# Three more weight remainders taken from PSUM, one weight copy moved ahead of the first convolution tap, a Silu moved behind a bank copy, loads issued ahead of stores, and one matrix's operand parts prepared a pair earlier

## The chip, the cores and the metric

The kernel runs on one core of a Trainium2 chip. The metric is device time in microseconds for one execution. A core has five instruction queues that run beside each other and wait for each other through semaphores: PE (TensorE, matrix products), DVE (VectorE), ACT (ScalarE), POOL (GpSimd) and SP (SyncE, which here issues all transfers of the steady part). Each queue runs its instructions in the order in which they were issued. Matrix products go into PSUM, which has eight banks of 128 x 512 float32 values; everything else lives in SBUF or in device memory.

## The reference

The input x has 1024 rows of 1024 float32 values. With one layer only the gated short convolution runs:

```python
def short_conv_mixer(u, w_in, conv_w, w_out):
    z, bg, cg, v = jnp.split(u @ w_in.astype(u.dtype), 4, axis=-1)
    y = bg * causal_dwconv(cg * v, conv_w) * jax.nn.silu(z)
    return y @ w_out.astype(u.dtype)

u = rms_norm(h, pre_norm[i])
h = h + rms_norm(m, post_norm[i])
```

w_in is 1024 x 8192 (four parts of 2048 columns), the causal convolution has three taps and works on each of the 2048 columns by itself, and w_out is 2048 x 1024. All of it is float32.

## The kernel before, in words

The kernel works transposed: columns of the projection lie on the 128 partitions and the 1024 positions lie along the free dimension. It has a start (normalisation, transposes, the operands made from u), a long first phase (the input projection, the gates and the convolution) and a second phase (the output projection and the last norm). The change touches the first phase.

**Channels and pairs.** The 2048 branch columns are sixteen channels c = 0 to 15 of 128 columns. A channel is two pairs: the even pair p = 2c is (CG, V), the odd pair p = 2c + 1 is (Z, BG). A pair is a 2 x 2 block product over halves of the contraction and halves of the positions, done by a seven-product scheme, products a to g. A product is four contraction tiles times three matmuls (low part of the weight by high part of the operand, high by low, high by high), so twelve matmuls of 128 x 512, in `product` (L221 to L223).

**Seven products inside.** From channel 3 on, product b, and for channels 4 to 14 product f too, is itself replaced by seven half-size products a' to g' (`deep_product`, L780 to L782, six matmuls of 128 x 256 each). `by_seven` says where: "f" from DEEP_F = 4 to channel 14. The half-size operands of f, c', e', d' and g', are made once from the operand of f, in three steps: `deep_parts` (L701, POOL adds the high and low part), `deep_subs` (L707 to L710, POOL subtractions) and `deep_split` (a copy to the high part on ACT, a subtraction to the low part on DVE, L160 and L161). The table UNDER says behind which product of which pair each step is issued.

**Splitting weights.** Each weight is split into a high part and a remainder. `split` copies on ACT (L160, L168) and subtracts on DVE with both inputs in SBUF (L161, L187). `split_by_bank` (L181 to L183) does one more ACT copy, of the source into one fixed PSUM bank named `beside`, and DVE subtracts with that bank as its first input. There is only one such bank, so the next ACT copy into it waits until DVE has read the last one. `split_w` and BY_BANK_DEEP choose between the two; names are wa to wg for the weights of a pair (dwb0 to dwb2, dwf0 to dwf2 for the half-size ones), with h or l behind for the two parts.

**What sets the order.** The list `slots` is the order of products on PE. Behind each product the loop issues, by hand, the splits of the weights that are due within LEAD = 7.0 us of planned time (`prepare`), then the reading of the bank (`after`, `deep_after`, `deep_after_f`), then loads, sums on POOL and the table UNDER. Every engine's order follows from this one program order. In an odd pair of channels 4 to 14 PE's order is c; c' and e' of f; e; f' of b and of f; d' of b and of f; d; g' of b and of f; then product a of the next pair; then g.

**What reads a bank.** Products a, c, d and g of a pair share one bank (px). Behind a and c, ACT copies the bank to SBUF (`snap`, L229), and PE may go on with the bank only then. Behind d, DVE adds the bank to a copy (L248), and g waits for that. In the half-size products DVE reads the banks at L787, L802, L812 and L816.

**Around the first tap.** Behind d' of b in an odd pair, `deep_after` adds the bank (L787), `gate` writes the gated input (L271, DVE), and `first_tap` scales it on ACT (L657). The two other taps are `conv_tap` (L666, DVE). Behind g' of f, `deep_after_f` adds the bank (L802, DVE), applies Silu (L806, ACT) and multiplies (L807, POOL). Behind a of the following even pair, ACT copies the bank (L229) and applies Silu to the other half (L1061).

**Stores and loads on SP.** `add_t` prepares the output projection's weights: DVE subtractions (L345, L332 to L340), each followed by a store that waits for it. `fetch_t` loads them, and `fetch_s` loads an earlier channel's result y for `add_y` (L302 to L304, from channel 9 on). TODO says at which pair which of these is done; before, it covers pairs 8 to 23, that is channels 4 to 11.

Of the kernel before, what the change touches and what calls it, by code (L numbers as in the profile page):

```python
# [17 lines left out]
DEEP_F = 4  # L18
LEAD = 7.0
BY_BANK_DEEP = (("b", 0), ("b", 1), ("f", 0))  # L20
# [3 lines left out]
def kernel(  # L24
# [16 lines left out]
    nc = tc.nc  # L41
# [147 lines left out]
    def split_w(p, kinds):  # L189
        for i in kinds if p < len(PAIRS) else "":  # L190
            if i in ("ag" if p % 2 else "adg") and by_seven("f", p // 2):
                wt[p, i] = [page(f"w{i}{h}_{p}", F32R) for h in "hl"]
                split_by_bank(source(p, i), *wt[p, i])
                continue
            split_high(p, i)
            split_low(p, i)
# [587 lines left out]
    def deep_after(c, i):  # L784
# [3 lines left out]
        if i == "d'":  # L788
            if by_seven("f", c):
                gate(c)  # L790
                first_tap(c)
            else:
                start_conv(c, lambda: third_unit(1) if c == NC - 1 else None)

    def deep_after_f(c, i):
# [4 lines left out]
        if i in ("b'", "g'"):  # L800
            t, v_ = (t0, banks[p, "v"]) if i == "b'" else (t1, banks[p + 1, "v"])
            nc.vector.tensor_add(t, v_, t)  # L802
            if i == "b'":
                nc.gpsimd.tensor_mul(g[:, :HH], t[:, :HH], sn[p, "e"][:, :HH])
            else:
                nc.scalar.activation(t, t, AF.Silu)  # L806
                nc.gpsimd.tensor_mul(cvs[c][:, HB:], t, sn[p + 1, "e"])  # L807
# [126 lines left out]
    TODO = {2 * DEEP_F + 2 * j + n: j + n * CH for j in range(CH) for n in (0, 1)}  # L934
# [3 lines left out]
    for p in range(2, len(PAIRS)):  # L938
# [32 lines left out]
        ("d", 2 * DEEP_F - 2): lambda: deep_parts("f", [0]),  # L971
        ("f", 2 * DEEP_F - 2): lambda: deep_parts("f", [2]),
        ("g", 2 * DEEP_F - 2): lambda: deep_parts("f", [1]),
        ("c", 2 * DEEP_F - 1): lambda: deep_parts("f", [3]),
        ("e", 2 * DEEP_F - 1): lambda: deep_subs("f", [0]),
        ("f", 2 * DEEP_F - 1): lambda: deep_subs("f", [1]),
        ("c", 2 * DEEP_F): lambda: deep_split("f", "c'"),
        ("d", 2 * DEEP_F): lambda: deep_split("f", "e'"),
        ("a", 2 * DEEP_F + 1): lambda: deep_split("f", "d'"),
        ("g", 2 * DEEP_F): lambda: deep_split("f", "g'"),  # L980
# [21 lines left out]
    for n, slot in enumerate(slots):  # L1002
# [21 lines left out]
        if i == "c":  # L1024
            if p % 2 and p // 2 < DEEP:
                nc.scalar.activation(sn[p, "a"], sn[p, "a"], AF.Silu)
            if p % 2 == 0 and p in TODO:
                add_t(TODO[p], [0, 1])
                fetch_t(TODO[q])
            if p % 2 == 0 and p > 2:  # L1030
                fetch_s(prev)
            if p % 2 == 0 and p // 2 >= DEEP:
# [26 lines left out]
        elif i == "a":  # L1059
            if prev >= 0 and p % 2 == 0 and by_seven("f", prev):  # L1060
                nc.scalar.activation(sn[p - 1, "a"], sn[p - 1, "a"], AF.Silu)  # L1061
# [264 lines left out]
```

## Time and profile before

| | us |
|---|---|
| median of three runs | 819.88 (818.24 to 820.08) |
| profiled execution | 818.51 |
| its span on the core | 816.7 |
| PE busy in the span | 780.3 (96%) |
| DVE busy | 675.2 (83%) |
| ACT busy | 399.6 (49%) |
| POOL busy | 401.9 (49%) |

The profile lists every instruction with its start and duration in microseconds from the start of the span. A bracket at the end of a row says how long the engine had been idle before it and what ended that. Matmuls overlap each other, so a matmul's own duration is longer than the distance to the next one; the pace of PE is read from the starts. "PEclk" is the share of full clock that TensorE was granted.

### The profile page before, as it was taken

The page shows a single profiled execution, that of the slowest core. Times are in us where ns is not written, and L with a number is a line of the kernel's source. Part 1 is how long each engine was busy: PE and PEld are TensorE (multiplying, and loading weights), DVE is VectorE, ACT ScalarE, POOL GpSimd, SP SyncE. Part 2 cuts the span into 40 slices and gives each one's busy share as a digit, 9 for nine tenths or more (in the row PEclk, how much of TensorE's full clock was granted, in tenths as well). Part 3 has the DMA queues.
Part 4 walks back from the last instruction along what each step waited for, and adds up shares of the span by engine and source line. Part 5 has one row for each costly group of instructions (what it writes and reads, how often), then busy time and mean ns, then how long its engine had stood idle before and what let it go on. Part 6 is the DMA issues. An engine that isn't in the chain of part 4 may idle for free.

```text
span 816.7 us, 11954 instructions
## 1 busy us (share of the span) xinstructions
PE 780.3 (96%) x4050; PEld 663.9 (81%) x4050; DVE 675.2 (83%) x964; ACT 399.6 (49%) x742; POOL 401.9 (49%) x337
## 2 busy tenths in 40 slices
PE   8999999998899999999898899999999999999997
PEld 6888888887787878787787777878787889989985
DVE  6899658979797979797978797768687899996885
ACT  7655425254445454445343443544544555855831
POOL 2516679678374747474645463838374210530031
PEclk9999999999999999999999999999999999999999
DMA  9212240515272717272828271415150989786445
GB/s 312 51 52 60 83 141 1 181 61 179 76 230 74 251 53 251 63 240 79 276 60 265 83 251 53 143 52 157 37 180 32 307 289 369 280 262 204 153 154 182
DMA packets 115822, 127.18 MB, mean 156 GB/s; under 512 B 7416, under 2 KB 74032, under 8 KB 115760
## 3 DMA queue, kind: packets, MB, share of 16 engines
q1 hardware_dynamic: 115744, 126.41, 47.9%
q8 instruction: 32, 0.52, 0.3%
q14 instruction: 30, 0.25, 0.1%
q10 hardware_dynamic: 16, 0.00, 0.0%
HBM read 91.78 MB, written 34.60 MB: 155 GB/s over the span
## 4 chain that ended last, share of the span: by engine, by line
PE 62%; DVE 19%; issue 9%; POOL 4%; ACT 4%; DMA 3%; DVEq 0%; POOLq 0%; SPq 0%; ACTq 0%
PE px L221 8%; PE px L222 7%; PE px L223 7%; PE po_x L1115 4%; PE po_x L1116 4%; PE po_x L1117 4%; PE pv L221 3%; PE pv L223 3%; PE pv L222 3%; DVE cv L666 3%; DMA s<-y_d 2%; DVE t L345 1%; ACT beside L182 1%; DVE sna L787 1%; DVE wel L187 1%
## 5 line engine op out<-in xcount | busy, mean ns | idle before, releaser
L252 POOL TENSOR_TENSOR sne<-sne,cv 128x512 f32<-128x512 f32 x15 | 20.9, 1393 | 156.8 <-DVE cv L666 147.6
L221 PE MATMUL px<-u_c,wcl 128*128 128x512 f32 x124 | 49.7, 401 | 12.8 <-DVE wcl L187 6.7
L182 ACT COPY beside<-raw 128x512 f32<-128x512 f32 x66 | 38.9, 589 | 28.4 <-DVE dwb1l L183 16.6
L187 DVE TENSOR_TENSOR wel<-se,weh 128x512 fp32r<-128x512 f32 x31 | 37.0, 1193 | 19.1 <-ACT weh L168 19.1
L229 ACT COPY snc<-px 128x512 f32<-128x512 f32 x31 | 18.2, 586 | 69.7 <-PE px L223 69.7
L221 PE MATMUL px<-u_g,wgl 128*128 128x512 f32 x124 | 49.4, 398 | 2.7 <-DVE sne L248 2.7
L154 POOL TENSOR_TENSOR sc<-se,raw 128x512 f32<-128x512 f32 x31 | 49.5, 1596 | 2.6 <-POOL se L152 0.2
L152 POOL TENSOR_TENSOR se<-raw,raw 128x512 f32<-128x512 f32 x31 | 45.4, 1463 | 10.6 <-DMA raw<-in_sc_w_in 6.3
L221 PE MATMUL px<-u_d,wdl 128*128 128x512 f32 x124 | 49.3, 398 | 0.0
L148 POOL TENSOR_TENSOR raw<-raw,raw 128x512 f32<-128x512 f32 x31 | 49.3, 1590 | 0.0
L221 PE MATMUL pv<-u_e,wel 128*128 128x512 f32 x124 | 48.6, 392 | 0.7 <-DVE wel L187 0.7
L156 POOL TENSOR_TENSOR sf<-raw,sc 128x512 f32<-128x512 f32 x31 | 49.1, 1583 | 0.0
L222 PE MATMUL px<-u_d,wdh 128*128 128x512 f32 x124 | 48.9, 395 | 0.0
L223 PE MATMUL px<-u_d,wdh 128*128 128x512 f32 x124 | 48.8, 393 | 0.0
L221 PE MATMUL px<-u_a,wal 128*128 128x512 f32 x124 | 48.6, 392 | 0.0
L222 PE MATMUL px<-u_a,wah 128*128 128x512 f32 x124 | 48.5, 391 | 0.0
L222 PE MATMUL px<-u_g,wgh 128*128 128x512 f32 x124 | 48.5, 391 | 0.0
L223 PE MATMUL px<-u_c,wch 128*128 128x512 f32 x124 | 48.4, 390 | 0.0
L222 PE MATMUL pv<-u_e,weh 128*128 128x512 f32 x124 | 48.4, 390 | 0.0
L223 PE MATMUL px<-u_g,wgh 128*128 128x512 f32 x124 | 48.3, 390 | 0.0
L222 PE MATMUL px<-u_c,wch 128*128 128x512 f32 x124 | 48.3, 389 | 0.0
L223 PE MATMUL pv<-u_e,weh 128*128 128x512 f32 x124 | 48.3, 389 | 0.0
(535 smaller groups left out, 2766.1 us busy)
## 6 DMA issues: line engine op xcount, KB each, us to landing
raw<-in_sc_w_in SPq DMA_DIRECT2D x128, 256.0 KB, 4.2
y_d<-cv SPq DMA_DIRECT2D x16, 512.0 KB, 3.0
s_d<-s SPq DMA_DIRECT2D x32, 256.0 KB, 4.4
t<-in_sc_w_out SPq DMA_DIRECT2D x32, 256.0 KB, 3.3
t_d<-t SPq DMA_DIRECT2D x32, 256.0 KB, 2.4
tb<-in_sc_w_out SPq DMA_DIRECT2D x16, 256.0 KB, 3.9
s<-y_d SPq DMA_DIRECT2D x16, 256.0 KB, 4.7
xr<-in_x SPq DMA_DIRECT2D x16, 256.0 KB, 4.0
```

The source lines that it names most:

```text
L148: nc.gpsimd.tensor_sub(t, block(p, 0, 0), t)
L152: nc.gpsimd.tensor_add(t, block(p, 1, 0), block(p, 1, 1))
L154: nc.gpsimd.tensor_sub(t, sums[p, "e"], block(p, 0, 0))
L156: nc.gpsimd.tensor_sub(t, block(p, 0, 1), sums[p, "c"])
L182: nc.scalar.copy(b, src)
L187: nc.vector.tensor_sub(lo, source(p, i), hi.bitcast(F32))
L221: nc.tensor.matmul(ps, lo, UH[i][:, k], start=first and k == 0, stop=False, skip_group_check=True)
L222: nc.tensor.matmul(ps, hi, UL[i][:, k], start=False, stop=False, skip_group_check=True)
L223: nc.tensor.matmul(ps, hi, UH[i][:, k], start=False, stop=last, skip_group_check=True)
L1115: nc.tensor.matmul(ps, lo, u[:, 0, k], start=first, stop=False, skip_group_check=True)
L1116: nc.tensor.matmul(ps, hi, u[:, 1, k], start=False, stop=False, skip_group_check=True)
L1117: nc.tensor.matmul(ps, hi, u[:, 0, k], start=False, stop=last, skip_group_check=True)
```

## The change

Five edits, all in the order or the kind of the small work around the matmuls; PE's own order of products stays the same.

1. The remainders of dwb2, dwf2 and of wd in odd pairs, in channels 4 to 14, are made by `split_by_bank` in place of `split`. Each has one more ACT copy, and DVE reads PSUM.
2. The weight wg of an odd pair in channels 4 to 14 is split ahead of `gate` and `first_tap`; before, it came behind `first_tap`.
3. The Silu behind g' of f and the POOL product behind it are issued behind the copy of the bank of the next pair's product a.
4. In even pairs from `TODO`, `fetch_t` and `fetch_s` are issued ahead of `add_t`, and TODO begins two pairs (one channel) later: pairs 10 to 25.
5. The steps that make f's half-size operands are issued earlier: the sums on POOL in pairs 5 to 7, the splits behind products e, d, f and g of pair 7, in channel 3 (before, the sums in pairs 6 and 7, the splits in pairs 8 and 9, in channel 4).

```diff
-BY_BANK_DEEP = (("b", 0), ("b", 1), ("f", 0))
+BY_BANK_DEEP = (("b", 0), ("b", 1), ("b", 2), ("f", 0), ("f", 2))
...
-            if i in ("ag" if p % 2 else "adg") and by_seven("f", p // 2):
+            if i in "adg" and by_seven("f", p // 2):
...
             if by_seven("f", c):
+                split_w(2 * c + 1, "g")
                 gate(c)
                 first_tap(c)
...
-            else:
-                nc.scalar.activation(t, t, AF.Silu)
-                nc.gpsimd.tensor_mul(cvs[c][:, HB:], t, sn[p + 1, "e"])
             return
...
-    TODO = {2 * DEEP_F + 2 * j + n: j + n * CH for j in range(CH) for n in (0, 1)}
+    TODO = {2 * DEEP_F + 2 + 2 * j + n: j + n * CH for j in range(CH) for n in (0, 1)}
...
-        ("d", 2 * DEEP_F - 2): lambda: deep_parts("f", [0]),
-        ("f", 2 * DEEP_F - 2): lambda: deep_parts("f", [2]),
-        ("g", 2 * DEEP_F - 2): lambda: deep_parts("f", [1]),
-        ("c", 2 * DEEP_F - 1): lambda: deep_parts("f", [3]),
-        ("e", 2 * DEEP_F - 1): lambda: deep_subs("f", [0]),
-        ("f", 2 * DEEP_F - 1): lambda: deep_subs("f", [1]),
-        ("c", 2 * DEEP_F): lambda: deep_split("f", "c'"),
-        ("d", 2 * DEEP_F): lambda: deep_split("f", "e'"),
-        ("a", 2 * DEEP_F + 1): lambda: deep_split("f", "d'"),
-        ("g", 2 * DEEP_F): lambda: deep_split("f", "g'"),
+        ("d", 2 * DEEP_F - 3): lambda: deep_parts("f", [0]),
+        ("f", 2 * DEEP_F - 3): lambda: deep_parts("f", [2]),
+        ("d", 2 * DEEP_F - 2): lambda: deep_parts("f", [1]),
+        ("f", 2 * DEEP_F - 2): lambda: deep_parts("f", [3]),
+        ("g", 2 * DEEP_F - 2): lambda: deep_subs("f", [0]),
+        ("c", 2 * DEEP_F - 1): lambda: deep_subs("f", [1]),
+        ("e", 2 * DEEP_F - 1): lambda: deep_split("f", "c'"),
+        ("d", 2 * DEEP_F - 1): lambda: deep_split("f", "e'"),
+        ("f", 2 * DEEP_F - 1): lambda: deep_split("f", "d'"),
+        ("g", 2 * DEEP_F - 1): lambda: deep_split("f", "g'"),
...
             if p % 2 == 0 and p in TODO:
-                add_t(TODO[p], [0, 1])
                 fetch_t(TODO[q])
             if p % 2 == 0 and p > 2:
                 fetch_s(prev)
+            if p % 2 == 0 and p in TODO:
+                add_t(TODO[p], [0, 1])
...
             if prev >= 0 and p % 2 == 0 and by_seven("f", prev):
-                nc.scalar.activation(sn[p - 1, "a"], sn[p - 1, "a"], AF.Silu)
+                for t in (sn[p - 1, "c"], sn[p - 1, "a"]):
+                    nc.scalar.activation(t, t, AF.Silu)
+                nc.gpsimd.tensor_mul(cvs[prev][:, HB:], sn[p - 1, "c"], sn[p - 1, "e"])
```

## The prediction

> **What bounds the kernel now.** First PE's own list of waits, for a queue that is busy nearly throughout (us in total, times, longest).
>
> ```profile
> PE pv2f L780 <- DVE snc L816: 10.3, 7, 2.6
> PE px L221 <- DVE wcl L187: 6.7, 4, 2.3
> PE px L221 <- ACT sna L229: 6.0, 8, 0.8
> PE px L221 <- DVE sne L248: 2.7, 6, 0.7
> ```
>
> PE waits for late readers of a bank and for late remainders on DVE and ACT, and for little else. Then the stretches of channel 4, of 5 to 8, 9 to 11, 12, and 13 with 14, cut where product c of an even pair starts (length; PE, PEld, DVE, ACT, POOL busy; granted clock, DMA share, GB/s), and from the timeline the pace of matmuls that wait for nothing.
>
> ```profile
> 176.03:221.15 45.12, 39.60 (x205) 33.90 (x204) 39.77 (x57) 20.91 (x42) 28.75 (x26) 0.96 0.42 137
> 221.15:379.79 158.64, 152.52 (x817) 129.40 (x815) 137.70 (x197) 75.54 (x141) 93.07 (x77) 1.00 0.49 156
> 379.79:508.63 128.84, 117.68 (x613) 100.15 (x613) 109.16 (x154) 56.99 (x106) 69.14 (x58) 0.97 0.50 161
> 508.63:547.96 39.33, 37.92 (x206) 32.32 (x205) 29.52 (x44) 19.06 (x36) 21.53 (x20) 1.00 0.33 101
> 547.96:626.17 78.21, 75.86 (x408) 64.64 (x408) 58.69 (x87) 37.63 (x70) 43.91 (x39) 1.00 0.33 101
> sum 450.14, PE 423.58 PEld 360.40 DVE 374.85 ACT 210.14 POOL 256.38; mean PE 84.72 PEld 72.08 DVE 74.97 ACT 42.03 POOL 51.28
> ```
>
> ```profile
> 173.31 0.39 PE L221 MATMUL px<-u_g,wgl 128*128 128x512 f32 x1
> 176.03 0.39 PE L221 MATMUL px<-u_c,wcl 128*128 128x512 f32 x1
> ...
> 252.00 0.28 PE L780 MATMUL px2b<-ubgh_deep,dwb 128*128 128x256 f32 x1
> 252.35 0.28 PE L780 MATMUL px2b<-ubgh_deep,dwb 128*128 128x256 f32 x1
> ```
>
> A whole product, twelve matmuls, takes 176.03 - 173.31 = 2.72 us, and three half-width matmuls 0.35. A channel is ten products and 84 half-width matmuls: 27.2 + 9.9 = 37.1 us if PE waits for nothing. Eleven channels need 408.1 and take 450.1: 42.0 us are loss, 8.0 of it in channel 4, 10.2 in 5 to 8, 17.5 in 9 to 11, 2.2 in 12, 4.0 in 13 and 14. That is all that this change can win; PE's order stays, and so does the work of the start and of the second phase.
>
> **Silu and the tap (edits 2 and 3).** The turn from channel 5 to 6, in the timeline (start, us, engine, line; idle before and its end in brackets):
>
> ```profile
> 250.79 1.15 ACT L657 ACTIVATE cv<-gpad,cw 128x1024 f32<-128x1024 f32 x1 [3.01 <-issue]
> 252.97 0.69 DVE L183 TENSOR_TENSOR wgl<-beside,wgh 128x512 fp32r<-128x512 f32 x1 [2.26 <-ACT beside L182]
> 255.97 0.69 DVE L248 TENSOR_TENSOR sne<-px,sne 128x512 f32<-128x512 f32 x1
> 256.71 0.50 PE L221 MATMUL px<-u_g,wgl 128*128 128x512 f32 x1 [0.40 <-DVE sne L248]
> 258.81 0.63 ACT L806 ACTIVATE snc<-snc 128x512 f32<-128x512 f32 x1 [5.32 <-DVE snc L802]
> 259.86 0.58 ACT L229 COPY sna<-px 128x512 f32<-128x512 f32 x1
> 260.49 0.50 PE L221 MATMUL px<-u_c,wcl 128*128 128x512 f32 x1 [0.75 <-ACT sna L229]
> ```
>
> ACT stands 5.32 us at the Silu, and the bank copy that PE needs stands behind it. Product a ended before g began, over 3 us earlier; with the Silu behind the copy, PE doesn't wait. By the list that is 6.0 us in eight waits, and each costs PE some 0.16 more between starts: 7.3 us. Silu and the POOL product land 1 to 2 us later than the copy, and only the store of y waits for them; DVE's half of y is later still.
>
> ACT also idles 3.01 us ahead of the tap, so the two copies of wg (0.6 each) fit in there. DVE's gate comes 0.69 us later, the tap with it, but the 2.26 us of waiting for `beside` go: L248 at 255.97 would come some 1.6 us sooner, more than PE's wait of 0.40. Six such waits, 2.7 us in the list, 3.7 with the restarts, go. If the tap came later by more than that, they would stay.
>
> **Three more through PSUM (edit 1).** The groups of instructions by form (count, busy, mean ns):
>
> ```profile
> L161 DVE TENSOR_TENSOR dwf2l<-dsf,dwf2h 128x512 fp32r<-128x512 f32 x11 | 18.5, 1678 | 0.0
> L161 DVE TENSOR_TENSOR dwb2l<-dsb,dwb2h 128x512 fp32r<-128x512 f32 x13 | 17.7, 1358 | 0.0
> L187 DVE TENSOR_TENSOR wdl<-raw,wdh 128x512 fp32r<-128x512 f32 x20 | 25.7, 1287 | 4.5 <-ACT wdh L168 4.5
> L183 DVE TENSOR_TENSOR wdl<-beside,wdh 128x512 fp32r<-128x512 f32 x11 | 7.6, 691 | 7.4 <-ACT beside L182 7.4
> ```
>
> DVE saves 1.68 + 1.36 + 1.29 - 3 x 0.69 = 2.3 us a channel; ACT does three copies more, about 0.58 each as the bank copy at 259.86, 1.7 us, at half load. But the three follow each other, and one bank serves them: behind the first subtraction ACT makes the next copy, the snap of c, wdh and the third copy, each about 0.6, with the second subtraction beside them, so the third ends about 0.69 + 4 x 0.6 + 0.69 = 3.8 us after the first starts. Now channel 10:
>
> ```profile
> 432.33 0.86 SPq L289 DMA_DIRECT2D s<-y_d  x2
> 439.31 0.69 DVE L302 TENSOR_TENSOR s<-s,cv 128x512 f32<-128x512 f32 x1 [1.83 <-DMA s<-y_d]
> 442.61 0.47 PE L221 MATMUL px<-u_c,wcl 128*128 128x512 f32 x1 [2.17 <-DVE wcl L187]
> 446.92 1.44 DVE L161 TENSOR_TENSOR dwb2l<-dsb,dwb2h 128x512 fp32r<-128x512 f32 x1
> 452.01 0.41 DVE L816 TENSOR_TENSOR snc<-pv2f,snc 128x256 f32<-128x256 f32 x1
> 452.47 0.39 PE L780 MATMUL pv2f<-u_f,dwf2l 128*128 128x256 f32 x1 [1.97 <-DVE snc L816]
> ```
>
> The bank reader that PE waits for comes 452.01 - 446.92 = 5.1 us behind the first of the three; with 3.8 for them and 0.34 for the reader in between, 4.1. So each pv2f wait shrinks by 0.95. The longest of the seven, 2.6, is channel 4's and goes with the work that leaves it; of the three near 1.97 in channels 9 to 11 about 1.0 is left, 1.15 with the restart; the rest, 10.3 - 2.6 - 5.9 = 1.8 in channels 6 to 8, all but goes. Bounds: by busy time alone 2.3 a channel is won and these waits end; with the copies standing behind DVE's backlog nothing is won. I take the row of channel 10.
>
> **Loads ahead of stores (edit 4).** s<-y_d was issued at 432.33 behind two stores that waited for L345; it can go some 4 us earlier, and the 1.83 us wait at L302 ends. DVE then makes wcl 1.83 sooner, and 0.34 of PE's 2.17 is left. Of the 6.7 us of wcl waits 2.3 are channel 4's; the other 4.4 in channels 9 to 11 become about 0.45 each with restarts, as DVE has the same work there. If the loads land no sooner, all 4.4 stay. Channel 4 loses and channel 12 gains the weight preparation:
>
> ```profile
> L345 DVE TENSOR_TENSOR t<-t,t 128x512 f32<-128x512 f32 x32 | 39.9, 1265 | 0.3
> ```
>
> Four of these, 5.1 us, and four half-width ones. Channel 12 becomes like 9 to 11.
>
> **f's operand parts (edit 5).** The same sums now stand earlier on POOL, and the eight split steps (four pairs of copy and subtraction) in the end of channel 3:
>
> ```profile
> 154.55 1.67 POOL L260 TENSOR_TENSOR gpad<-snc,sne 128x512 f32<-128x512 f32 x1 [5.77 <-DVE snc L255]
> 164.79 0.69 DVE L183 TENSOR_TENSOR wal<-beside,wah 128x512 fp32r<-128x512 f32 x1 [1.94 <-ACT beside L182]
> 171.33 0.68 DVE L248 TENSOR_TENSOR sne<-px,sne 128x512 f32<-128x512 f32 x1
> 174.81 0.58 ACT L229 COPY sna<-px 128x512 f32<-128x512 f32 x1
> 179.60 0.71 ACT L160 CAST ufch_deep<-deepf 128x256 fp32r<-128x256 f32 x2
> 182.38 1.84 DVE L161 TENSOR_TENSOR ufcl_deep<-deepf,ufch_deep 128x256 fp32r<-128x256 f32 x2
> 208.81 0.42 PE L782 MATMUL px2b<-ubdh_deep,dwb2h 128*128 128x256 f32 x1
> 212.22 0.39 PE L221 MATMUL px<-u_d,wdl 128*128 128x512 f32 x1
> ```
>
> Three of POOL's four additions of 128x512 (about 1.67 each, as the product in the first row) come ahead of that row, at which POOL idles 5.77 us; what they push back, weight sums of pair 7, is covered by that, and I cost them nothing. Without the cover it would be their excess over 5.77, nothing to 1 us, at product c of pair 7.
>
> Of the splits, the first pair (1.84 on DVE) fills the idle 1.94. The next two stand between L248 and the snap at 174.81: 1.84 on DVE, 0.71 on ACT, 0.9 for the second half of a DVE pair and 0.4 for the bank reader (L787) that now comes behind it, 3.9 in all, and the Silu of channel 3 isn't moved out of the way there. PE's c of pair 8 had 0.64 us to spare after the snap; with what runs over from the first pair the new gap is 3.2 to 4.4, taken as 3.9.
>
> Such a gap costs more than itself. After the longest pv2f wait, 2.6 us, which ended at 207.75, the ten 256-column and three 512-column matmuls from 208.81 to 212.22 took 3.41 us where 10 x 0.117 + 3 x 0.227 = 1.85 is usual: 1.6 us lost, with the granted clock of that channel at 0.96. So the loss in channel 4 is 3.9 + 1.6 + 0.7 for restarts = 6.2, against 8.0.
>
> [...]
>
> **The sum.** Losses after. Channel 4: 6.2. Channels 5 to 8: 10.2 less four waits at the turn (0.91 each, 3.6), three for L248 (0.56 each, 1.7) and 2.0 of pv2f with restarts, 2.9. Channels 9 to 12: 0.45 + 1.15, and 0.8 for restarts and slow matmuls behind them, 2.4 each, 9.6. Channels 13 and 14: 4.0 less 1.8 and 1.3 at the turn, 0.9. Together 19.6; won are 42.0 - 19.6 = 22.4. On the profiled execution (818.51, span 816.7) that is 796.1; it lies 1.4 below the median, so I predict 797.5.
>
> **The rivals.**
> Everything goes: the copies find the bank free, no gap at channel 4, and 0.7 is left in every channel: loss 8, time 785. For it: DVE has 34 to 36 busy us in a channel of 37.1; against it: the chain up to 174.81.
> Only the turn is won: the single bank holds ACT and DVE back, and pv2f and wcl waits stay. Then 7.3 + 3.7 = 11.0, less 2 in channel 12, which gets 9 to 11's load: 811. For it: 7.4 us of DVE idle ahead of the eleven wdl that already come through the bank; against it: 3.8 us for three is less than 4.98 busy in channel 10 (the stretch 446.92 to 452.01 less one reader).
> Slower: ACT, standing at `beside` for a remainder that DVE makes late, holds the snap of c that product d of the odd pair needs. Between the end of c and d lie a half-size pair (1.4), e (2.7) and four half-size products (2.8); less the snap itself, 6.3 us are to spare. A DVE backlog beyond 6.3 us costs, one beyond 6.3 + 22.4 / 11 = 8.3 makes the kernel slower than before; at 9.5 each of eleven channels waits 3.2 more than forecast, 797.5 + 35 = 833. For it: the snap stands between the second and third copy in ACT's order. Against it: DVE itself stands only 1.97 us behind PE in channel 10.
> No change: a gap of over 20 us at channel 4 would eat it all, 818 to 822; only a chain several times that of the rows does that.
>
> **How the numbers follow.** About 0.3% (2.5 us) is what this measurement can tell from none. Chances: forecast 0.70; everything goes 0.08; only the turn 0.10; no change 0.04; slower 0.08. So faster 0.88, same 0.04, slower 0.08. The forecast's own range, 788 to 808, is from the bounds: 22.4 less 4 (edit 1 wins nothing in channels 9 to 12), 4.4 (wcl waits stay) and 2 (channel 4); or 22.4 with 4.6 (the pv2f waits end there) and 5 (no gap at channel 4), of which I take about all on each side. The range 786 to 811 adds the cases next to it and leaves out slower, unchanged and half of the best.
>
> **What would show it.** Right: the wait of PE for ACT's sna is gone but for one at about 178 to 181; Silu has no 5 us idle ahead of it; L666 follows the tap with no wait for `beside` ahead; dwb2l, dwf2l and wdl take 0.69; no DMA wait at L302; channel stretches of 38 us (5 to 8, 13, 14) and 39 to 40 (9 to 12). Wrong: pv2f gaps of 2 us still there, wcl late in channel 12, `beside` waits of several us on ACT with a late snap of c or a in each channel, or a gap above 5 us at channel 4.

## The result, and the profile after

The changed kernel takes 795.15 us (median; 794.17 to 795.50) against 819.48 for the kernel before on the same chips: 0.970 of the time, with a 95% interval from 0.969 to 0.972. The prediction was 797.5 us, in a range from 786 to 811. The profiled execution took 794.88 us with a span of 793.1.

PE's own list of waits after (us in total, times, longest):

```profile
PE px L221 <- ACT sna L229: 7.1, 1, 7.1
PE pv L221 <- DVE wfl L187: 2.3, 1, 2.3
PE pv2f L780 <- DVE snc L814: 1.9, 6, 0.4
```

The eight waits for the bank copy are one, of 7.1 us. The waits for L248 and for wcl are not in the list any more, and the seven pv2f waits of 10.3 us are six of 1.9 (L814 is L816 of the kernel before). A wait for wfl is new. By stages, with the stretch from c of pair 6 to c of pair 8 (most of channel 3) ahead of those of channel 4, 5 to 8, 9 to 11, 12, and 13 with 14 (columns as in the prediction); first that one stretch in the kernel before, then all six after:

```profile
138.00:176.03 38.03, 38.02 (x188) 31.94 (x186) 31.55 (x40) 15.66 (x31) 27.82 (x23) 1.00 0.34 104
```

```profile
137.70:186.89 49.19, 39.80 (x188) 32.87 (x186) 40.34 (x46) 17.10 (x36) 34.74 (x32) 0.94 0.20 59
186.89:226.24 39.35, 39.35 (x204) 33.98 (x205) 27.30 (x44) 21.55 (x41) 17.70 (x16) 0.95 0.34 101
226.24:376.64 150.40, 149.77 (x818) 130.04 (x816) 129.36 (x196) 83.94 (x154) 89.24 (x77) 1.00 0.52 165
376.64:490.22 113.58, 112.67 (x613) 97.58 (x612) 99.15 (x153) 62.66 (x115) 66.35 (x58) 1.00 0.60 192
490.22:528.07 37.85, 37.55 (x205) 32.51 (x204) 33.04 (x51) 20.90 (x39) 22.12 (x20) 1.00 0.51 164
528.07:602.68 74.61, 74.61 (x409) 64.95 (x408) 52.88 (x87) 41.33 (x76) 42.98 (x39) 1.00 0.35 106
```

With the 37.1 us that the prediction gave a channel without waits, the losses are:

| stretch | loss before | predicted | loss after |
|---|---|---|---|
| channel 3, above its 38.0 before | 0 | 0 (its gap counted below) | 11.2 |
| channel 4 | 8.0 | 6.2 | 2.3 |
| 5 to 8 | 10.2 | 2.9 | 2.0 |
| 9 to 11 | 17.5 | 7.2 | 2.3 |
| 12 | 2.2 | 2.4 | 0.8 |
| 13 and 14 | 4.0 | 0.9 | 0.4 |
| sum | 42.0 | 19.6 | 18.9 |

So the total came out within 1 us of the loss forecast, but through two errors that nearly cancel: channels 3 and 4 lose 13.4 where 6.2 was forecast, channels 5 to 14 lose 5.4 where 13.4 was. That the total was met is luck. Channels 13 and 14, in which PE doesn't wait, show that the floor itself is 74.61 / 2 = 37.3, so that channels 5 to 14 keep hardly any loss at all.

The turn from channel 9 to 10 after, from the timeline:

```profile
407.97 1.28 DVE L666 SCALAR_TENSOR_TENSOR cv<-gpad,cw,cv 128x1024 f32<-128x1024 f32 x1 [0.67 <-ACT cv L657]
409.77 0.68 DVE L248 TENSOR_TENSOR sne<-px,sne 128x512 f32<-128x512 f32 x1
411.93 0.59 ACT L229 COPY sna<-px 128x512 f32<-128x512 f32 x1 [2.96 <-PE px L223]
414.45 0.39 PE L221 MATMUL px<-u_c,wcl 128*128 128x512 f32 x1
```

DVE doesn't stand for wgl here any more: its idle time ahead of wgl is 3.6 us in the whole kernel, where it was 28.5. It waits 0.67 us for the tap instead. The copy at 411.93 now waits for PE and not PE for it, Silu follows it, and c starts without a wait.

The new loss, in the timeline of channel 3's end (DVE, ACT and PE):

```profile
176.00 0.69 DVE L248 TENSOR_TENSOR sne<-px,sne 128x512 f32<-128x512 f32 x1
176.60 1.85 DVE L161 TENSOR_TENSOR ufel_deep<-deepf,ufeh_deep 128x256 fp32r<-128x256 f32 x2
178.38 1.77 DVE L187 TENSOR_TENSOR wcl<-sc,wch 128x512 fp32r<-128x512 f32 x1
180.07 0.68 DVE L255 TENSOR_TENSOR snc<-pv,snc 128x512 f32<-128x512 f32 x1
180.78 0.63 ACT L257 ACTIVATE snc<-snc 128x512 f32<-128x512 f32 x1 [6.29 <-DVE snc L255]
181.32 0.69 ACT L160 CAST ufdh_deep<-deepf 128x256 fp32r<-128x256 f32 x2
181.74 2.75 DVE L161 TENSOR_TENSOR ufdl_deep<-deepf,ufdh_deep 128x256 fp32r<-128x256 f32 x2 [0.99 <-ACT ufdh_deep L160]
184.41 0.41 DVE L787 TENSOR_TENSOR sna<-px2b,sna 128x256 f32<-128x256 f32 x1
185.21 0.63 ACT L1012 ACTIVATE sna<-sna 128x512 f32<-128x512 f32 x1 [3.20 <-DVE sna L787]
...
186.26 0.58 ACT L229 COPY sna<-px 128x512 f32<-128x512 f32 x1
186.89 0.79 PE L221 MATMUL px<-u_c,wcl 128*128 128x512 f32 x1 [7.08 <-ACT sna L229]
```

DVE and ACT wait for each other by turns: a split of f's operand (ufel) and one of wcl on DVE, then L255, a Silu that waited 6.29 us for it, the copy for the third split behind that Silu, its subtraction on DVE, L787 behind it, the second Silu behind L787, and the bank copy that PE needs behind them all. From L248 to that copy it is 10.3 us where it was 174.81 - 171.33 = 3.5 before. Behind the gap, the next matmuls start 0.43 us apart (187.48, 187.91, 188.33) and not 0.23.

### The profile page after: what moved, and what is told of

Its sections match the earlier page's. It is cut to its first block, busy times and chain, and to the rows that moved or that the text cites. A ratio compares the mean times of both kernels' runs of the same rounds, so it can differ in the third digit from the quotient of the medians.

```text
span 793.1 us, 11970 instructions
## 1 busy us (share of the span) xinstructions
PE 773.6 (98%) x4050; PEld 664.7 (84%) x4050; DVE 649.9 (82%) x964; ACT 420.1 (53%) x775; POOL 392.4 (49%) x337
## 5 line engine op out<-in xcount | busy, mean ns | idle before, releaser
L182 ACT COPY beside<-raw 128x512 f32<-128x512 f32 x77 | 45.5, 590 | 31.6 <-DVE dwb1l L183 21.5
L229 ACT COPY sna<-px 128x512 f32<-128x512 f32 x30 | 17.6, 587 | 66.1 <-PE px L223 66.1
L152 POOL TENSOR_TENSOR se<-raw,raw 128x512 f32<-128x512 f32 x31 | 49.3, 1589 | 5.6 <-DMA raw<-in_sc_w_in 4.1
L666 DVE SCALAR_TENSOR_TENSOR cv<-gpad,cw,cv 128x1024 f32<-128x1024 f32 x32 | 42.2, 1319 | 11.4 <-ACT cv L657 11.2
L222 PE MATMUL px<-u_a,wah 128*128 128x512 f32 x124 | 48.5, 391 | 0.0
L223 PE MATMUL px<-u_a,wah 128*128 128x512 f32 x124 | 48.3, 389 | 0.0
L154 POOL TENSOR_TENSOR sc<-se,raw 128x512 f32<-128x512 f32 x31 | 46.0, 1485 | 2.4
L148 POOL TENSOR_TENSOR raw<-raw,raw 128x512 f32<-128x512 f32 x31 | 46.2, 1491 | 0.0
```

The costliest lines, as they stand in the source:

```text
L148: nc.gpsimd.tensor_sub(t, block(p, 0, 0), t)
L152: nc.gpsimd.tensor_add(t, block(p, 1, 0), block(p, 1, 1))
L154: nc.gpsimd.tensor_sub(t, sums[p, "e"], block(p, 0, 0))
L182: nc.scalar.copy(b, src)
L222: nc.tensor.matmul(ps, hi, UL[i][:, k], start=False, stop=False, skip_group_check=True)
L223: nc.tensor.matmul(ps, hi, UH[i][:, k], start=False, stop=last, skip_group_check=True)
```

## Experiments

All times are medians; each kernel was compared with the kernel before on the same chip (818.55 to 819.36 us there). Where two of the other kernels are compared, they may have run on different chips, between which the kernel before differs by up to 0.9 us.

### Without edit 5

```diff
-        ("d", 2 * DEEP_F - 3): lambda: deep_parts("f", [0]),
...
-        ("g", 2 * DEEP_F - 1): lambda: deep_split("f", "g'"),
+        ("d", 2 * DEEP_F - 2): lambda: deep_parts("f", [0]),
...
+        ("g", 2 * DEEP_F): lambda: deep_split("f", "g'"),
```

> The changed kernel without edit 5: the operand parts of f are made in channels 3 and 4, as in the kernel before; the other four edits stay. In the changed kernel the stretch from c of pair 6 to c of pair 8 takes 186.89 - 137.70 = 49.2 us where it took 176.03 - 138.00 = 38.0 before: 11.2 us more, and about 2 us of slow matmuls follow. Theory: edit 5 causes these, and in channel 4, which edit 4 has freed of four weight subtractions (5.1 us on DVE), the splits find room. Then the gaps of 2.47 us at product f of pair 6 and of 7.24 us at c of pair 8 go, channel 4 loses 2 to 4 us, and the time is 783 to 787. Rival one, the prediction's size of it: edit 5 costs about 6 us less what channel 4 loses in its place, 789 to 793. Rival two: the splits cost the same wherever they stand, and PE waits in channel 4 what it now waits in channel 3: 794 to 797.

Measured: 784.63 us (783.98 to 784.78), 0.957 of before (0.956 to 0.959). Theory. Edit 5 costs 10.5 us of the 34.7 that the other four win. PE waits for neither wfl nor the bank copy in channel 3 any more. Channel 4, where the splits now lie, takes 40.07 us, 0.7 more than the 39.35 of the changed kernel, which hold the slow matmuls behind its gap.

### The two halves of edit 5

Sums early, splits late:

```diff
-        ("e", 2 * DEEP_F - 1): lambda: deep_split("f", "c'"),
-        ("d", 2 * DEEP_F - 1): lambda: deep_split("f", "e'"),
-        ("f", 2 * DEEP_F - 1): lambda: deep_split("f", "d'"),
-        ("g", 2 * DEEP_F - 1): lambda: deep_split("f", "g'"),
+        ("c", 2 * DEEP_F): lambda: deep_split("f", "c'"),
+        ("d", 2 * DEEP_F): lambda: deep_split("f", "e'"),
+        ("a", 2 * DEEP_F + 1): lambda: deep_split("f", "d'"),
+        ("g", 2 * DEEP_F): lambda: deep_split("f", "g'"),
```

> The changed kernel with the four splits of f's operand parts back at their places in channel 4, and the POOL sums and subtractions left early as edit 5 has them; this parts edit 5 in two. Without edit 5 altogether the kernel took 784.63. Theory: the gap of 2.47 us at product f of pair 6, with some 1.7 us of slow matmuls behind it, is from the sums, the gap of 7.24 us at c of pair 8 is from the splits; so the first stays and the second goes: 787.5 to 790. Rival one: the early sums also push the weight sums of pair 7 and 8, so c of pair 8 stays late by some 2 us too: 790 to 793. Rival two: neither is from the sums: 784 to 786.

Measured: 785.60 us (783.95 to 785.91), 0.959 (0.957 to 0.961). The waits are as the theory says, the sum isn't: the wait for wfl stays (2.3 us) and the one for the bank copy is gone, but channel 4 takes only 37.30 us, where it took 40.07 with the sums late. The early sums cost 3.8 us in channel 3 and win 2.8 in channel 4, which none of the three expectations had; rival two has the number without the reason. The traces show where the 2.8 come from. Without edit 5 POOL still makes four of f's subtractions in channel 4 (177.76 to 181.40 us); DVE then waits 1.44 us for POOL's weight sums (L738), and wel takes 1.45 us beside POOL. With the sums early that wait is gone, and wel takes 0.68. The stretches of channel 3 and of channel 4 in this kernel:

```profile
137.79:179.58 41.79, 39.46 (x188) 33.01 (x187) 32.47 (x40) 15.98 (x31) 30.71 (x27) 0.96 0.24 70
179.58:216.88 37.30, 37.30 (x205) 32.47 (x204) 31.09 (x49) 22.70 (x46) 22.93 (x21) 1.00 0.35 106
```

### Channel 3's Silus behind the copy as well

```diff
-                nc.scalar.activation(t, t, AF.Silu)
-                nc.gpsimd.tensor_mul(cvs[c][:, HB:], t, sn[p, "e"])
+                if c != DEEP:
+                    nc.scalar.activation(t, t, AF.Silu)
+                    nc.gpsimd.tensor_mul(cvs[c][:, HB:], t, sn[p, "e"])
...
-            elif i == "g'" and not by_seven("f", c):
+            elif i == "g'" and not by_seven("f", c) and c != DEEP:
...
-            if prev >= 0 and p % 2 == 0 and by_seven("f", prev):
+            if prev >= 0 and p % 2 == 0 and (by_seven("f", prev) or prev == DEEP):
```

> The changed kernel with channel 3's two applications of Silu, and the POOL product behind the first, also behind the copy of the bank of product a of pair 8, as edit 3 has it from channel 4 on. On ACT that copy (186.26) stood behind a Silu that waited 6.29 us for DVE (L255) and one that waited 3.20 us (for L787). Theory: in-order ACT behind DVE is what made the 7.24 us gap, and most of it goes; what is left is DVE's own lateness with the weight wcl (its subtraction ended at 180.15, PE was ready at 179.65), 0.5 us, and 1 to 2 us at wel, for which the fourth split on DVE stands ahead: 787 to 790. Rival: DVE's work itself is what is too much there; wel takes the place of the copy and PE stands as long one product later: 792 to 795.

Measured: 787.35 us (787.28 to 790.60), 0.963 (0.960 to 0.965). Theory: with all of edit 5 in place, moving the two Silus wins 7.8 us. PE's list has a 0.5 us wait for wcl, 0.4 for wel and 0.8 for dwf0l in place of the 7.1, so DVE's work was late by about that and the order on ACT made the rest. Channel 3 takes 41.09 us.

### Each of the other edits alone

Edit 1 alone (the first two changes in the diff):

```diff
-BY_BANK_DEEP = (("b", 0), ("b", 1), ("f", 0))
+BY_BANK_DEEP = (("b", 0), ("b", 1), ("b", 2), ("f", 0), ("f", 2))
-            if i in ("ag" if p % 2 else "adg") and by_seven("f", p // 2):
+            if i in "adg" and by_seven("f", p // 2):
```

> The kernel before with edit 1 alone: three more remainders of a channel taken from PSUM. Theory, by the prediction's terms: 0.95 us less at each pv2f wait, 0.5 to 2 us of channel 4, and nothing at the turn or at wcl: 813 to 817. Rival one: DVE, 2.3 us less busy in a channel, is ahead everywhere, and the waits for wcl and L248 shrink as well: 805 to 812. Rival two: the one bank orders ACT behind DVE's backlog, and what DVE wins is waited out: 819 to 822.

Measured: 812.74 us (811.70 to 813.76), 0.992 (0.991 to 0.994). Just below the theory's range: of the pv2f waits 2.3 us in three are left. What the theory didn't have: the waits for L248 and for the bank copy grew, to 5.5 us and 8.4 us in eleven each, so a part of what pv2f won was lost again at the turn.

Edit 2 alone:

```diff
             if by_seven("f", c):
+                split_w(2 * c + 1, "g")
                 gate(c)
```

> The kernel before with edit 2 alone: the weight wg split ahead of the gate and the first tap. Theory, the prediction's size: six waits of PE for L248, 2.7 us and 3.7 with what follows, go, and the waits for the bank copy stay: 815 to 817. Rival one: the copies of wg hold the tap back, the two other taps on DVE come later and the waits for L248 stay: 819 to 821. Rival two: edit 2 wins little alone, since the Silu behind it holds PE at c in any case and what g wins is lost there: 818 to 820.

Measured: 802.44 us (801.02 to 805.33), 0.980 (0.978 to 0.983). None of the three: 16.6 us, over four times the 3.7 that the prediction gave this edit. PE's list has no wait for L248 and none for the bank copy, although Silu still stands ahead of the copy. The turn from channel 5 to 6 in this kernel (that of the kernel before stands in the prediction):

```profile
252.65 0.68 DVE L248 TENSOR_TENSOR sne<-px,sne 128x512 f32<-128x512 f32 x1
...
254.39 0.39 PE L221 MATMUL px<-u_g,wgl 128*128 128x512 f32 x1
254.78 0.68 DVE L803 TENSOR_TENSOR snc<-pv,snc 128x512 f32<-128x512 f32 x1
255.49 0.64 ACT L807 ACTIVATE snc<-snc 128x512 f32<-128x512 f32 x1 [4.17 <-DVE snc L803]
256.54 0.58 ACT L229 COPY sna<-px 128x512 f32<-128x512 f32 x1
257.17 0.50 PE L221 MATMUL px<-u_c,wcl 128*128 128x512 f32 x1
```

L248 starts 1.74 us ahead of g, where it stood 0.74 ahead of it with PE waiting. Silu starts 1.10 us behind g's start, where it was 258.81 - 256.71 = 2.10 before, so the copy behind it ends just when PE comes to c. The late Silu was itself an effect of DVE's standing at wgl: one cause, which the prediction had booked as two. Both bookings together are 11.0 us, though, and not 16.6. What they leave out is the clock: in the profiled execution of the kernel before, the granted clock falls to 0.50 for 3.41 us three times in channels 4 to 14 (from 208.79, 410.18 and 495.51 us), here only once, in channel 4 (a mean of 0.96 from 175.84 to 219.46 us, and 1.00 in every later stretch). By the prediction's 1.6 us for such a spell that is some 3.2 us; the other 2.4 were not traced to single waits.

Edit 3 alone:

```diff
-            else:
-                nc.scalar.activation(t, t, AF.Silu)
-                nc.gpsimd.tensor_mul(cvs[c][:, HB:], t, sn[p + 1, "e"])
...
-                nc.scalar.activation(sn[p - 1, "a"], sn[p - 1, "a"], AF.Silu)
+                for t in (sn[p - 1, "c"], sn[p - 1, "a"]):
+                    nc.scalar.activation(t, t, AF.Silu)
+                nc.gpsimd.tensor_mul(cvs[prev][:, HB:], sn[p - 1, "c"], sn[p - 1, "e"])
```

> The kernel before with edit 3 alone: Silu and the POOL product behind the copy of the next product a. Theory: eight waits of PE for the bank copy, 6.0 us and 7.3 with what follows them, end, and nothing else stands behind them: 812 to 813. Rival one: the next late one, DVE's L248 or the weight wcl, takes the place of the copy, and half or less of it is won: 816 to 819. Rival two: more than 7.3 is won, since the store of y and the loads behind it do not matter but a late c pushed everything behind it: under 811.

Measured: 807.62 us (806.29 to 808.59), 0.986 (0.984 to 0.987), 11.7 us: rival two by the number. The waits for the copy are gone, those for L248 are 3.3 us in five. Here too only one of the three spells at half clock is left, in channel 4 (a mean of 0.96 from 175.74 to 219.63 us, and 1.00 in every later stretch), and 7.3 + 3.2 = 10.5 of the 11.7 us come out that way; the rival's own reason isn't shown.

Edit 4 alone:

```diff
-    TODO = {2 * DEEP_F + 2 * j + n: j + n * CH for j in range(CH) for n in (0, 1)}
+    TODO = {2 * DEEP_F + 2 + 2 * j + n: j + n * CH for j in range(CH) for n in (0, 1)}
...
-                add_t(TODO[p], [0, 1])
                 fetch_t(TODO[q])
             if p % 2 == 0 and p > 2:
                 fetch_s(prev)
+            if p % 2 == 0 and p in TODO:
+                add_t(TODO[p], [0, 1])
```

> The kernel before with edit 4 alone: loads ahead of stores, and the weight preparation two pairs later. Theory, by the prediction's terms: channel 4 loses less by about 2 us, the wcl waits in channels 9 to 11 (4.4 us) all but end, channel 12 loses about 2 more: 815 to 817. Rival one: with the late load gone DVE is also less late at the reader of pv2f, so more than 4 us is won there too: 810 to 814. Rival two: the loads land no sooner, or DVE's load alone makes wcl late, and only the move from channel 4 to 12 is left: 819 to 821.

Measured: 814.14 us (813.80 to 815.10), 0.994 (0.992 to 0.995): 1 us better than the theory, though not for rival one's reason, since the pv2f waits are 13.4 us in nine, no less than before. PE's waits for wcl fell to 1.7 us in four, 0.4 each, which is the 0.34 that the prediction left of 2.17.

The four together win 34.7 us, alone they win 6.6, 16.6, 11.7 and 5.2, about 40 in all. Most of the excess is the clock again. The profiled executions have three spells at half clock in channels 4 to 14 before, two each with edit 1 or 4 alone, one each with edit 2 or 3 alone, and none with the four together (mean clocks with edit 1 alone 0.96 in channel 4 and 0.99 in 9 to 11, with edit 4 alone 0.97 in 9 to 11, with the four 1.00 in every stretch). Singly that is six fewer, together only three; the other three, at 1.6 us, are 4.8 of the 5.5 us of excess.

### The changed kernel without edit 1

> The changed kernel without edit 1: the three remainders are made from SBUF again. What edit 1 brings with the others in place. The prediction's size: 0.95 us at each of the pv2f waits, 2 us in channels 5 to 8 and about 4 in 9 to 12: 800 to 802. Theory, after the run of edit 1 alone, in which three waits of 2.3 us in all were left of seven with 10.3: the whole of each pv2f wait bar 0.5 us is edit 1's, 1 us in each of channels 5 to 8 and 1.6 in each of 9 to 12, and wcl is late again in channels 9 to 12 by 0.5: 804 to 808. Rival: with the turn and the loads out of the way DVE catches up by itself and edit 1 brings under 3 us: 795 to 798.

The edit is the reverse of edit 1's diff. Measured: 799.40 us (797.99 to 800.10), 0.977 (0.975 to 0.978): 4.25 us more than the changed kernel, below both the theory and the prediction's size, above the rival's. wcl isn't late again; only pv2f is, 6.5 us in six where the changed kernel has 1.9 in six. In company the other edits have already taken part of what edit 1 takes alone. The subtractions from SBUF in this kernel, and the reader that PE waits for behind them (channel 9):

```profile
396.83 1.45 DVE L161 TENSOR_TENSOR dwb2l<-dsb,dwb2h 128x512 fp32r<-128x512 f32 x1
398.21 1.78 DVE L161 TENSOR_TENSOR dwf2l<-dsf,dwf2h 128x512 fp32r<-128x512 f32 x1
...
402.41 0.39 PE L780 MATMUL pv2f<-u_f,dwf2l 128*128 128x256 f32 x1 [1.40 <-DVE snc L814]
```

and the same place in the changed kernel:

```profile
398.35 0.68 DVE L183 TENSOR_TENSOR dwb2l<-beside,dwb2h 128x512 fp32r<-128x512 f32 x1
399.05 0.59 ACT L182 COPY beside<-dsf 128x512 f32<-128x512 f32 x1 [5.70 <-DVE dwb2l L183]
399.68 0.69 DVE L183 TENSOR_TENSOR dwf2l<-beside,dwf2h 128x512 fp32r<-128x512 f32 x1 [0.66 <-ACT beside L182]
401.20 0.69 DVE L183 TENSOR_TENSOR wdl<-beside,wdh 128x512 fp32r<-128x512 f32 x1 [0.83 <-PE pv L221]
402.14 0.42 DVE L814 TENSOR_TENSOR snc<-pv2f,snc 128x256 f32<-128x256 f32 x1
402.61 0.39 PE L780 MATMUL pv2f<-u_f,dwf2l 128*128 128x256 f32 x1 [0.27 <-DVE snc L814]
```

DVE idles 0.66 and 0.83 us ahead of the second and third, so the one bank does set the pace, and a little faster than worked out: the third ends 401.20 + 0.69 - 398.35 = 3.5 us after the first starts, forecast were 3.8, and the reader comes 402.14 - 398.35 = 3.8 us after it, forecast were 4.1. (The bracket at wdl names PE; the copy into the bank ended at 401.17, just before.)

### Edits 1, 2 and 4 without 3

> Edits 1, 2 and 4 alone: the changed kernel without edit 5 (784.63 us) and now without edit 3 too, so Silu is again ahead of the bank copy. Alone, edit 2 gave 802.44 and edit 3 807.62, 16.6 and 11.7 us under the kernel before, and the trace of edit 2 alone has no wait of PE for L248 and none for the copy. Theory: both act on one chain. Edit 2 ends DVE's wait for the bank beside, so that L802 and with it Silu come in time, and the copy behind Silu is no longer late; edit 3 is then worth nothing: 784 to 786. Rival, the prediction's sum: each edit ends waits of its own, and 7.3 us come back in eight to eleven waits for the copy: 791 to 796.

The edit is that of edit 3 alone, taken back. Measured: 791.54 us (791.41 to 792.76), 0.967 (0.966 to 0.969). The theory falls: edit 3 is worth 6.9 us even when edit 2 is there. But the rival is right only in the number, not in the place. PE's waits for the bank copy are 0.4 us in two; it is pv2f (5.6 us in seven, 3.8 in seven with edit 3) and wcl (1.6 in four, none with edit 3) that come back. The reason is in these rows of this kernel:

```profile
405.50 0.63 ACT L807 ACTIVATE snc<-snc 128x512 f32<-128x512 f32 x1 [4.17 <-DVE snc L803]
406.04 0.60 ACT L168 CAST weh<-se 128x512 fp32r<-128x512 f32 x1
406.68 1.44 DVE L187 TENSOR_TENSOR wel<-se,weh 128x512 fp32r<-128x512 f32 x1 [1.21 <-ACT weh L168]
```

Silu, released by DVE, stands ahead of weh, for which DVE then idles 1.21 us; PE notices some products later. In the groups, that idle time of DVE ahead of wel is 19.1 us in this kernel, as in the kernel before, and 5.8 with edit 3 added (first row this kernel, second the changed kernel without edit 5):

```profile
L187 DVE TENSOR_TENSOR wel<-se,weh 128x512 fp32r<-128x512 f32 x31 | 37.9, 1222 | 19.1 <-ACT weh L168 19.1
```

```profile
L187 DVE TENSOR_TENSOR wel<-se,weh 128x512 fp32r<-128x512 f32 x31 | 35.3, 1140 | 5.8 <-ACT weh L168 5.8
```

### Is POOL's idle time free?

Three kernels with edits 1 to 4, the splits in channel 4, and the sums at third places. First, three sums into POOL's idle time behind d of pair 6:

```diff
-        ("d", 2 * DEEP_F - 3): lambda: deep_parts("f", [0]),
-        ("f", 2 * DEEP_F - 3): lambda: deep_parts("f", [2]),
-        ("d", 2 * DEEP_F - 2): lambda: deep_parts("f", [1]),
+        ("d", 2 * DEEP_F - 2): lambda: deep_parts("f", [0, 2, 1]),
```

> The changed kernel with f's operand parts at third places: three of the sums on POOL behind product d of pair 6 and one behind f, so that they fall into the 5.77 us in which POOL idles ahead of L260; the subtractions behind g of pair 6 and c of pair 7, and the splits in channel 4 as in the kernel before. With all of it late (edit 5 undone) the kernel took 784.63, with the sums early and the splits late 785.60. Theory: the early sums lost 4 us at product f of pair 6, since the weight sums dsb stood behind them on POOL, and won about 3 us in channel 4, where POOL then had less left to do beside the splits; in the idle time they lose nothing and still win it: 781 to 783. Rival: they lose as much, as they push back the sum of the weights of pair 7 that stands behind L260, or the win in channel 4 is not from them: 784 to 788.

Measured: 784.07 us (783.98 to 784.19), 0.958 (0.956 to 0.959): in the rival's range. Channel 4 does take 37.45 us, so the win there is from POOL's sums and subtractions being done by then; the wait for wfl is gone; but a new one of 1.5 us stands at product a of pair 7.

Then one more remainder from PSUM:

```diff
-            if i in "adg" and by_seven("f", p // 2):
+            if i in ("adeg" if p % 2 else "adg") and by_seven("f", p // 2):
```

> The same with one edit more: the remainder of we in odd pairs of channels 4 to 14 also comes from PSUM. In the changed kernel that subtraction (L187 at 396.64) took 1.45 us beside a POOL addition, and the gap at pv2f, 0.43 to 0.52 us in six channels, stands behind it on DVE. Theory: 0.69 in place of 1.45 ends those gaps, about 2.7 us: 778 to 781. Rival: the one bank is taken once more, between dwb2 and what stands ahead of it, and ACT behind DVE makes the next remainders later; pv2f waits grow or weights come late: 782 to 790.

Measured: 782.39 us (782.29 to 782.51), 0.956 (0.954 to 0.957). 1.7 us of the 2.7 expected were won: pv2f waits are 0.4 us in two. The number lies in the rival's range, but the rival's growth of pv2f isn't there. The theory's range was too low, since it was set from a frame that came out 1 to 3 us slower than expected.

Last, one sum behind d, three behind f and g:

```diff
-        ("d", 2 * DEEP_F - 2): lambda: deep_parts("f", [0, 2, 1]),
-        ("f", 2 * DEEP_F - 2): lambda: deep_parts("f", [3]),
-        ("g", 2 * DEEP_F - 2): lambda: deep_subs("f", [0]),
-        ("c", 2 * DEEP_F - 1): lambda: deep_subs("f", [1]),
+        ("d", 2 * DEEP_F - 2): lambda: deep_parts("f", [0]),
+        ("f", 2 * DEEP_F - 2): lambda: deep_parts("f", [2, 1]),
+        ("g", 2 * DEEP_F - 2): lambda: deep_parts("f", [3]),
+        ("c", 2 * DEEP_F - 1): lambda: deep_subs("f", [0]),
+        ("e", 2 * DEEP_F - 1): lambda: deep_subs("f", [1]),
```

> The changed kernel with the PSUM remainder of we added, and f's operand parts between the earlier places: one POOL sum behind product d of pair 6, as in the kernel before, the other three behind f and g, the subtractions behind c and e of pair 7, the splits in channel 4. With three sums behind d in the same frame the kernel took 782.39, and there DVE's two subtractions ubgl took 2.94 us beside the sums where they took 1.83 without them, wal 1.75 where it took 0.68, and PE waited 1.63 us at product a of pair 7. Theory: POOL's work is no free filler of POOL's idle time, it slows the subtractions that DVE makes from SBUF at that moment; with the sums taken out of that stretch ubgl takes 1.8, wal 0.7, and the wait at a goes: 780.5 to 782, if the sums at their new place disturb nothing that PE waits for. Rival: DVE was late there for another reason, or the same slowing comes back at wfl or wel of pair 7 and channel 4 waits again: 782.4 to 785.

Measured: 780.95 us (780.67 to 781.37), 0.954 (0.952 to 0.955). Theory. This kernel is 14.2 us faster than the changed one. The same place in the timeline, with three sums behind d (first; the second of these three kernels) and with one (second; the last):

```profile
146.98 4.51 POOL L701 TENSOR_TENSOR deepf<-u_f 128x512 f32<-128x512 f32 x3 [0.36 <-DVE ubdl_deep L161]
147.43 2.94 DVE L161 TENSOR_TENSOR ubgl_deep<-deepb,ubgh_deep 128x256 fp32r<-128x256 f32 x2
150.29 1.75 DVE L187 TENSOR_TENSOR wal<-raw,wah 128x512 fp32r<-128x512 f32 x1
152.09 0.50 PE L221 MATMUL px<-u_a,wal 128*128 128x512 f32 x1 [1.48 <-DVE wal L187]
```

```profile
147.54 1.66 POOL L701 TENSOR_TENSOR deepf<-u_f 128x512 f32<-128x512 f32 x1 [0.37 <-DVE ubdl_deep L161]
147.98 1.84 DVE L161 TENSOR_TENSOR ubgl_deep<-deepb,ubgh_deep 128x256 fp32r<-128x256 f32 x2
149.74 0.68 DVE L187 TENSOR_TENSOR wal<-raw,wah 128x512 fp32r<-128x512 f32 x1
```

wal takes 1.75 us beside POOL's sums and 0.68 once POOL is done. The two ubgl take 2.94 us where POOL works throughout, and 1.84 where its single sum ends at 149.20, while they run; ubgl's difference is 1.10, wal's 1.07. The subtractions with an input in PSUM took 0.67 to 0.69 us throughout, with POOL at work or not (88 at L183 in the kernel before, 121 in the changed one).

## Why the prediction was right, and where it wasn't

**The turn (edits 2 and 3).** The mechanism was right: both kinds of waits went, and the rows look as announced. The sizes were wrong in the booking. The prediction took 7.3 us for Silu and 3.7 for the tap, as two separate sums. Alone the edits win 11.7 and 16.6 us. The step that failed is "ACT stands 5.32 us at the Silu, and the bank copy that PE needs stands behind it" as the whole of that wait's cause: DVE was late for the Silu because it had stood 2.26 us at wgl, and edit 2 alone ends both waits of PE. What edit 3 adds then lies elsewhere, at wel on DVE, and is seen at pv2f and wcl (6.9 us, kernel without edit 3). And the spells at half clock behind PE's waits, 1.6 us each, were in no term of the turn.

**Three more through PSUM (edit 1).** Right in mechanism, and near in pace (3.5 us for the three, not 3.8). The 0.95 us for each wait were too few: for this edit alone the waits in channels 9 and 11 fell from 1.98 and 1.97 us to 0.69 and 0.68, and as the last one added it takes 1.40 to 0.27 at the wait shown (4.25 us in all). What was left of these waits was put at about 1.0 us in channels 9 to 12 and is at most 0.4: besides the mis-sized 0.95, the sum hadn't what the other edits win for DVE there, which bring these waits from 1.97 to 1.40 without edit 1.

**Loads ahead of stores (edit 4).** Right for the edit alone, 0.4 us left of each wcl wait. In company nothing was left: with edits 1, 2 and 4 it was still 1.6 us in four, and adding edit 3 ended it. In channel 10 of the changed kernel the load for L302 was issued at 420.07, and L302 at 428.73 waits for no transfer:

```profile
428.73 0.68 DVE L302 TENSOR_TENSOR s<-s,cv 128x512 f32<-128x512 f32 x1
```

Channel 12, put at 2.4 us of loss, has 0.8. So the mis-sized term is "2.4 each, 9.6" for channels 9 to 12: it measured 3.0 in all.

**f's operand parts (edit 5).** Two steps failed. "What they push back, weight sums of pair 7, is covered by that, and I cost them nothing": the wait for wfl, 2.3 us, came earlier, in pair 6, and it goes when the first sums come behind d of pair 6. The two sums put ahead (from 134.64 and 139.23 us) keep POOL at work for longer beside DVE: the subtractions for u_b take 2.95 us at 138.04 where they took 1.84, and that for wfl takes 1.75 where it took 0.68. That makes 2.2 of the 2.3 us (first row before, second after):

```profile
146.96 0.68 DVE L187 TENSOR_TENSOR wfl<-sf,wfh 128x512 fp32r<-128x512 f32 x1
```

```profile
147.91 1.75 DVE L187 TENSOR_TENSOR wfl<-sf,wfh 128x512 fp32r<-128x512 f32 x1
```

Ahead of POOL's idle 5.77 us there was no room for them, and within it DVE's subtractions took longer beside them (2.94 us in place of 1.84 for the two ubgl, 1.75 in place of 0.68 for wal). The other step is "3.9 in all" for the chain up to the bank copy: it grew by 10.3 - 3.5 = 6.8 us, because the third split's subtraction went fully into it (2.75 and not 0.9), wcl took 1.77 us and not 0.7, and two round trips between DVE and ACT stood in it where one was counted. Moving the two Silus out of it won 7.8 us. The prediction had named the Silu of channel 3 as still in the way and a gap above 5 us there as a sign of error. That sign came.

**Slow matmuls behind a gap.** The prediction let a gap of 3.9 us cost 1.6 more; behind the 7.1 us wait channel 4 shows 39.35 where it takes 37.3 without, 2.0 us. Behind the wait of 2.3 us for wfl it came out either way: in the changed kernel slow matmuls follow it, with channel 3's Silus moved none do (granted clock 1.00 from 137.91 to 179.00 us). The granted clock changes at 208.79, 212.20, 410.18, 413.59, 495.51, 498.92 and 812.95 us in the trace before, and at 150.05, 153.46, 184.18, 191.01 and 791.75 in the trace after; within each of the two, these times lie whole multiples of 3.413 us apart. Here are the 3.41 us ahead of 150.05 and those behind it in the changed kernel, then 3.41 us with most of that wait in the kernel with the Silus moved (length; PE, PEld, DVE, ACT, POOL busy; granted clock, DMA share, GB/s):

```profile
146.63:150.05 3.42, 1.10 (x5) 0.65 (x4) 3.42 (x4) 0.00 (x0) 2.79 (x3) 1.00 0.97 271
150.05:153.46 3.41, 3.41 (x9) 2.65 (x9) 3.31 (x6) 1.14 (x2) 1.09 (x1) 0.50 0.43 117
```

```profile
148.34:151.75 3.41, 1.73 (x8) 1.46 (x9) 3.41 (x4) 1.14 (x2) 2.40 (x2) 1.00 0.98 282
```

In the changed kernel the whole wait, 147.48 to 149.80, lies in the first of these stretches, PE idles 2.3 us of it, and the next one runs at 0.50. With the Silus moved PE idles 1.7 us of the stretch shown, up to 150.02, and the clock stays at 1.00 behind it; that a step of that spacing begins at 148.34 there, within the wait, is the author's estimate, as the clock doesn't change near it. Cut in step with the changes of the clock, the trace before has three stretches from 20 us to the end of channel 14 in which PE idles about 2.0 us or more (2.4, 2.0 and 2.0), the trace after three (2.3, 3.4 and 2.7). Behind each of these six the clock is 0.50 for the next 3.413 us; behind all others, with 1.7 us of idle PE or less, it is 1.00. What sets the clock these traces don't show. For the prediction this means that its 1.6 us behind a gap was no matter of the gap's length alone.

**The rivals.** "Everything goes" was right for channels 5 to 14, where 5.4 us are left, and wrong at channel 4 only; with edit 5 undone it gives 784.63, beside the 785 worked out. "Only the turn" fell: pv2f and wcl waits went too. (The 4.98 us that it names are the three subtractions, 1.44, 1.78 and 1.76; the stretch less one reader is 4.7.) "No change" fell, as the gap at channel 4 is 7.1 us and not over 20. "Slower" fell: ACT does stand 5.70 us at the bank, but the copy of c behind it kept nothing waiting at d. The chances for "only the turn" and "slower", 0.10 and 0.08, leaned on the fear that copies in order behind DVE must hold something up; they did only where several round trips lie in one chain.

## What to carry to other kernels

When several edits work on one in-order chain, take each wait back to its first cause before adding: a wait that stands behind another one's delay goes with that one, and the slack that an edit gives an engine shows up at waits that it doesn't touch. Idle time of POOL was no free room here for sums that read SBUF beside DVE subtractions with two SBUF inputs (1.75 us in place of 0.68 for wal): look for a place for such work where DVE reads PSUM (0.67 to 0.69 us with POOL at work or not) or has time. Follow a chain that alternates between two in-order engines instruction by instruction, and count the round trips. Where gains of single edits add up to more than the edits win together, look whether each of them ends the same spells at half clock (here three before, none with the four edits together).

## What the runs showed of the hardware that was not expected

A DVE subtraction of 128x512 with both inputs in SBUF took 0.68 us alone and 1.75 to 1.78 us beside POOL in the rows shown, a factor of 2.6, while one with an input in PSUM took 0.67 to 0.69 in either case. And a wait of PE for wfl was followed by 3.41 us at a granted clock of 0.50 in the changed kernel (from 150.05 us), and by none with channel 3's Silus moved (1.00 from 137.91 to 179.00 us). In the 3.413 us up to 150.05 PE idled 2.3 us; of the stretches of this length in the traces before and after, cut in step with the changes of the clock, none with 1.7 us of idle PE or less was followed by half clock from 20 us to the end of channel 14.
